# A decoder trunk on one core: the first up pair of the MLP in the wide form

## Chip, cores and metric

One core of a Trainium2 chip runs the whole program. The metric is device time in microseconds (us). The kernel before took 1468.94 us (median of 3 runs, 1468.91 to 1469.76).

## What is computed

Two decoder layers on 512 tokens of width 1024, all in 32-bit floats, and a last RMSNorm. In each layer an attention branch and a retention branch are merged, and an MLP follows. The change is in the MLP:

```python
def hybrid_layer(x, g_mix, w_in, sinks, w_a, w_b, w_out, g_mlp, w_up, w_down):
    ...
    x = x + mixed @ w_out
    h2 = rmsnorm(x, g_mlp)
    x = x + jnp.square(jax.nn.relu(h2 @ w_up)) @ w_down     # w_up: 1024 x 4096
    return x
```

## The kernel before

Activations lie with features on the partitions and the 512 tokens along the free dimension. The 32-bit product is made of three matmuls on split numbers: each operand is `hi` (a rounded copy, made by ScalarE) plus `lo` (the rest, made by VectorE), and hi·hi, hi·lo and lo·hi are summed in PSUM (`products`, L332 to L334).

**Weights.** They come in units of 128x1024 from one long list. `unit()` hands over the next one and has the two behind it split already: SyncE loads `raw` (L196, or L219 for the parked pairs), ScalarE makes `hi` (L286), VectorE makes `lo` (L287). `raw`, `hi` and `lo` have three buffers each. So a `hi` can only be made when TensorE has read the `hi` that held its buffer, and a `raw` can only be loaded when the `lo` of the unit before it in that buffer has been made.

**The up product.** The 32 chunks of 128 columns of w_up go so: four in one `group` (four PSUM banks, full width), then fourteen pairs of chunks. A pair computes a 2x2 block product with seven block products in place of eight (a Strassen form): blocks are 512 features by 256 tokens. It takes four units, and holds three PSUM banks named b, a and e, in this order: a from an input block; b starts as a copy of a; e from a sum of blocks ("form"); b and a each go on accumulating; b and e each once more; b a last time, for which its readers must be done. Each of these seven products is called a multiply below: four pieces of 128 rows.

There are two forms of the pair. `narrow_pair` writes 256 columns per matmul, three matmuls per piece (12 per multiply). `wide_pair` puts the moving hi and lo side by side as 512 columns: one matmul of 512 columns with the weights' hi (L1356 before the change) and one of 256 with their lo (L1357), so 8 matmuls per multiply. It leaves two halves in PSUM that must be added: copies of e and b are 512 wide (`eu`, L1386, and `bu`, L1390, ScalarE), the copy of a into b too (L1383), and `join` and `join_copied` add the halves on VectorE (L1362 and L1363, L1367 to L1369). Then VectorE applies relu and the RMS factor to all 512 tokens of both chunks (L1409), ScalarE squares (L1429), and the result is split (L339, L340).

`pair` picks the form by the chunk number c = 8q + 2i with `wide(c)`. Before, `FIRST_WIDE` is 6: the first pair of a layer (c = 4) is narrow and the other thirteen are wide. The first wide pair on the second PSUM pool (c = 8) starts with one matmul more (L1381), which writes the whole bank b once. The four chunks of the group are still in PSUM when the first pair begins: they need the RMS factor `rstd` (L464 to L472), which is only ready then. Their evacuation (L1333, L1334, then the split L339 and L340) is handed to the first pair, whose steps issue it between its own (`late`).

**Order.** A scheduler of the build orders the instructions of each engine; on the chip each engine takes them in that order. The pairs of one layer and the down products between them (`two_chunks`, which use the squared results) are interleaved by it.

Of the kernel before, what the change touches and what calls it, by code (L numbers as in the profile page):

```python
# [14 lines left out]
ALU = mybir.AluOpType  # L15
# [3 lines left out]
P = 128  # L19
# [29 lines left out]
DEEP = 3  # L49
DELAY = 2  # L50
ASIDE = 48
FIRST_WIDE, LAST_WIDE = 6, 32
BETWEEN = (0, 2, 4, 5)
PARKED = (("w_b", 0), ("w_b", 2), ("w_out", 6), ("w_up", 4), ("w_up", 6))
H = T // 2
# [37 lines left out]
def wide(chunk):  # L93

    return FIRST_WIDE <= chunk < LAST_WIDE
# [32 lines left out]
def decoder(ctx, tc, xT, x_first, w_in, w_a, w_b, w_out, w_up, w_down, tables, decay, band, triangles, g_last, out):  # L128
    nc = tc.nc
# [13 lines left out]
    def temp(name="t"):  # L143
        return tmp.tile([P, T], F32, tag="t", name=name)

    def big(name, dtype=F32):
        return tmp.tile([P, 2, T], dtype, tag="big", name=name, bufs=7)

    def bank(pool, name):
        return pool.tile([P, T], F32, tag=pool.name, name=name)  # L150
# [141 lines left out]
    def unit(name, layer):  # L292
        i = state["next"]
        assert order[i][:2] == (layer, name), (order[i], layer, name)
        state["next"] += 1
        split_until(i + 3)
        return parts.pop(i)
# [28 lines left out]
    def products(ps, pairs, start, stop, resume=False):  # L326


        n = len(pairs)
        for i, ((ah, al), (bh, bl)) in enumerate(pairs):  # L330
            more = {"skip_group_check": True} if resume else {}
            nc.tensor.matmul(ps, ah, bh, start=start and i == 0, stop=False, **more)  # L332
            nc.tensor.matmul(ps, ah, bl, start=False, stop=False, **more)  # L333
            nc.tensor.matmul(ps, al, bh, start=False, stop=stop and i == n - 1, **more)  # L334

    def split(hi, lo, src, scale=None):

        if scale is None:
            nc.scalar.activation(hi, src, AF.Copy)  # L339
            nc.vector.tensor_tensor(lo, src, f32(hi), ALU.subtract)  # L340
        else:
            nc.scalar.activation(hi, src, AF.Copy, scale=scale)  # L342
            nc.vector.scalar_tensor_tensor(lo, src, scale, f32(hi), ALU.mult, ALU.subtract)
# [58 lines left out]
    def all_of(steps):  # L402
        for step in steps:
            step()
# [198 lines left out]
    def layer_body(layer):  # L603
        g_mix, g_mlp = 2 * layer, 2 * layer + 1
        rms_mix, rms_mlp = Rms(g_mix, True), Rms(g_mlp, False)
# [4 lines left out]
        def forms_home():  # L610

            t = slots.four()
            form = t[0].rearrange("p a (b t) -> p (a b) t", t=H).rearrange("p (j k s) t -> p j k s t", k=2, s=2)
            return t, form
# [27 lines left out]
        def form_of(by_form):  # L642
            return lambda j: [by_form[2 * (j // 2) + k // 2][:, j % 2, k % 2, :, :] for k in range(4)]

        def block(half, tokens):
            at = slice(tokens * H, tokens * H + H)
            return [x_homes[k // 2][0][:, k % 2 :: 2, at] for k in range(4 * half, 4 * half + 4)]
# [3 lines left out]
        def narrow_pair(pool, step, form, block, put):  # L651
            def multiply(ps, weights, left, moving, start=True):
                hi, lo = weights
                cols = [slice((0 if left else 4 * P) + k * P, (0 if left else 4 * P) + (k + 1) * P) for k in range(4)]
                pairs = [((hi[:, c], lo[:, c]), m if isinstance(m, tuple) else (m[:, 0, :], m[:, 1, :])) for c, m in zip(cols, moving)]
                products(ps, pairs, start, True, not start)

            b, a, e = (bank(pool, "mm")[:, :H] for _ in range(3))
            eu, z = temp("eu"), big("z")
            part = unit("pair", layer)  # L660
            multiply(a, part, True, block(0, 0))
            ins = nc.scalar.activation(b, a, AF.Copy).ins
            step(ins)
            multiply(e, part, False, form(0))
            ins = nc.scalar.activation(eu[:, :H], e, AF.Copy).ins
            step(ins)
            part = unit("pair", layer)
            multiply(b, part, True, form(1), False)
            ins = nc.scalar.activation(eu[:, H:], b, AF.Copy).ins
            step(ins)  # L670
            multiply(a, part, False, block(1, 0), False)
            step(put(0, FIRST, a, z).ins)
            part = unit("pair", layer)
            multiply(b, part, True, form(2), False)
            ins = nc.vector.tensor_tensor(z[:, 1, SECOND], b, eu[:, :H], ALU.add).ins
            step(ins)
            multiply(e, part, False, block(1, 1), False)
            ins = nc.vector.tensor_tensor(z[:, 0, SECOND], e, eu[:, H:], ALU.add).ins
            step(ins)
            part = unit("pair", layer)  # L680
            multiply(b, part, True, form(3), False)
            put(slice(0, 2), SECOND, z[:, :, SECOND], z)
            put(1, FIRST, b, z)
            return z
# [474 lines left out]
        for u in range(4):  # L1159
            hi, lo = unit("w_a", layer)  # L1160
            for j in range(2):
                c = 2 * u + j
# [144 lines left out]
        for c in range(2, KD, 2):  # L1307
            pool = ps_mm if c == 4 else ps_aux
# [6 lines left out]
            slots.give(*t[1])  # L1315


        def positive(i, at, src, z):
            factor = rms_mlp.value[:, at]
            if not isinstance(i, int):  # L1320
                factor = factor.unsqueeze(1).broadcast_to([P, 2, H])
            return nc.vector.scalar_tensor_tensor(z[:, i, at], src, 0.0, factor, ALU.max, ALU.mult)

        homes_x = [forms_home() for _ in range(4)]
        by_form = [h[1] for h in homes_x]
        form = form_of(by_form)
# [13 lines left out]
        def up_home():  # L1340

            if any(len(f) == 4 for f in slots.free):
                t, own = slots.four()
                return t[:, 0:2, :], t[:, 2:4, :], own
            return big("uhi", F32R), big("ulo", F32R), []
# [66 lines left out]
        def pair(q, i, late):  # L1412

            c = 8 * q + 2 * i
            pool = ps_aux if i % 2 == 0 else ps_mm
            turn = iter(range(7))

            def step(ins):
                now = next(turn)
                while late and now == BETWEEN[4 - len(late)]:  # L1420
                    with tc.issue_after(ins), tc.issue_after(last_low[0]):
                        late.pop(0)()

            z = wide_pair(c == FIRST_WIDE + 2, i == 0 and q > 1, pool, step) if wide(c) else narrow_pair(pool, step, form, block, positive)
            all_of(late)
            late.clear()
            hi, lo, own = up_home()
            for i in range(2):
                nc.scalar.activation(z[:, i, :], z[:, i, :], AF.Square)  # L1429
                split(hi[:, i, :], lo[:, i, :], z[:, i, :])  # L1430
                up[q].append((hi[:, i, :], lo[:, i, :]))
            up_slots[q].extend(own)
# [52 lines left out]
    for layer in range(DEPTH):  # L1485
        layer_body(layer)
# [181 lines left out]
```

## Time and profile before

| | |
|---|---|
| median of 3 runs | 1468.94 us (1468.91 to 1469.76) |
| span of the profiled execution | 1467.5 us |
| TensorE busy (matmuls) | 1461.0 us, 100% |
| VectorE busy | 1161.6 us, 79% |
| ScalarE busy | 814.6 us, 56% |
| DMA, mean | 135 GB/s |

The profiled execution's own time is its span; the runs' median lies 1.4 us above it, for what lies around the program. How to read the rows: PE is TensorE, PEld its weight loads, DVE is VectorE, ACT is ScalarE, SPq is the queue of SyncE that issues the DMAs. A row of the timeline has the start in us, the length in us, engine, line, operation, output<-input, shape, and xN where N like instructions were merged. L12 is line 12 of the kernel. Lengths overlap: the next instruction of an engine starts before the last one's length is over, so what an instruction costs in a full queue is the distance from one start to the next. A matmul's end is modelled. In what follows that distance is called its step.

The two layers run the same program, so places come in twos. The first pair of the first layer lies at 423.6 to 436.4 us, that of the second 727.9 us later.

### The profile page before, as it was taken

Reading aid. Unit: us, or ns where it says so; the run is one execution under the profiler, and the core shown is the slowest. Engines: PE = TensorE matmul, PEld = TensorE weight load, DVE = VectorE, ACT = ScalarE, POOL = GpSimd, SP = SyncE. Lnnn points to the kernel's source line nnn. Section 1 sums busy time; section 2 is a strip of 40 time slices with the busy share of each in tenths; the row PEclk is TensorE's granted clock in tenths of the full one; section 3 lists DMA queues with packets and bytes.
Section 4 is the critical chain, followed back from the end, with each engine's and each line's share of the span. In section 5 each row is a group of like instructions: output and inputs, shape, how many; then the busy total and the mean of one; then the engine's idle time right before and its main releaser. Section 6 shows DMA issues by size and latency. Waiting matters only on the chain.

```text
span 1467.5 us, 20166 instructions
## 1 busy us (share of the span) xinstructions
PE 1461.0 (100%) x7434; PEld 1246.4 (85%) x7434; DVE 1161.6 (79%) x1912; ACT 814.6 (56%) x1306; POOL 3.7 (0%) x14
## 2 busy tenths in 40 slices
PE   9999999999999999999999999999999999999998
PEld 7888888888988888888888888888989888888887
DVE  7998778678988787776678977786899877877774
ACT  7657356654684445444456653666547754455544
POOL 0000000000000000000000000000000000000000
PEclk9999999999999999999999999999999999999999
DMA  6423843356443332333543258323654432333373
GB/s 227 134 87 101 280 166 98 104 171 210 130 120 125 101 115 88 107 108 115 165 121 102 86 168 285 107 95 107 191 197 123 144 101 87 125 105 101 108 200 108
DMA packets 73346, 198.65 MB, mean 135 GB/s; under 512 B 8712, under 2 KB 8864, under 8 KB 73248
## 3 DMA queue, kind: packets, MB, share of 16 engines
q1 hardware_dynamic: 72960, 196.84, 42.5%
q8 instruction: 58, 0.95, 0.3%
q10 hardware_dynamic: 288, 0.52, 0.1%
q14 instruction: 40, 0.33, 0.1%
HBM read 173.73 MB, written 20.98 MB: 133 GB/s over the span
## 4 chain that ended last, share of the span: by engine, by line
PE 99%; DVE 0%; issue 0%; POOLq 0%; ACT 0%; DVEq 0%; ACTq 0%
PE mm L334 24%; PE mm L332 23%; PE mm L333 23%; PE mm L1356 11%; PE mm L1357 6%; PE rv L332 2%; PE rv L334 2%; PE rv L333 2%; PE score L864 1%; PE r L332 1%; PE r L334 1%; PE r L333 1%; PE pT L819 0%; PE pv L846 0%; PE pv L845 0%; PE warm L311 0%
## 5 line engine op out<-in xcount | busy, mean ns | idle before, releaser
L333 PE MATMUL mm<-r,hi 128*128 128x512 f32 (+1 forms) x1568 | 572.5, 367 | 0.0
L332 PE MATMUL mm<-r,hi 128*128 128x512 f32 (+1 forms) x1568 | 569.9, 367 | 0.0
L334 PE MATMUL mm<-r,lo 128*128 128x512 f32 (+1 forms) x1568 | 563.9, 367 | 0.2
L286 ACT ACTIVATE hi<-raw 128x1024 fp32r<-128x1024 f32 (+1 forms) x334 | 333.9, 1002 | 377.8 <-PE mm L333 206.9
L287 DVE TENSOR_TENSOR lo<-raw,hi 128x512 fp32r<-128x512 f32 (+1 forms) x335 | 384.3, 1150 | 110.8 <-ACT hi L286 109.4
L334 PEld LDWEIGHTS mm<-r,lo 128*128 128x128 f32 x1568 | 293.6, 188 | 48.8 <-DVE lo L287 1.4
L332 PEld LDWEIGHTS mm<-r,hi 128*128 128x128 f32 x1568 | 294.1, 188 | 46.5 <-ACT r L342 0.2
L333 PEld LDWEIGHTS mm<-r,hi 128*128 128x128 f32 x1568 | 294.3, 188 | 46.0
L1356 PE MATMUL mm<-r,hi 128*128 128x512 f32 x728 | 252.0, 391 | 0.0
L1357 PE MATMUL mm<-r,lo 128*128 128x256 f32 x728 | 200.3, 277 | 0.0
L1356 PEld LDWEIGHTS mm<-r,hi 128*128 128x128 f32 x728 | 136.5, 188 | 28.7 <-ACT mm L1383 0.2
L1357 PEld LDWEIGHTS mm<-r,lo 128*128 128x128 f32 x728 | 136.7, 188 | 3.2 <-DVE lo L287 0.6
L1429 ACT ACTIVATE z<-z 128x512 f32<-128x512 f32 x56 | 32.5, 624 | 51.8 <-DVE z L1409 51.8
L1436 DVE TENSOR_TENSOR x<-x,mm 128x512 f32<-128x512 f32 x56 | 37.7, 686 | 28.1 <-PE mm L334 28.1
L334 PE MATMUL rv<-hi,r 128*128 128x512 f32 x128 | 49.8, 389 | 0.0
L333 PE MATMUL rv<-lo,r 128*128 128x512 f32 x128 | 49.8, 389 | 0.0
L332 PE MATMUL rv<-hi,r 128*128 128x512 f32 x128 | 49.8, 390 | 0.0
L339 ACT ACTIVATE r<-z 128x512 fp32r<-128x512 f32 x64 | 38.5, 619 | 16.3 <-DVE z L1090 16.1
L340 DVE TENSOR_TENSOR r<-z,r 128x512 fp32r<-128x512 f32 x64 | 42.9, 685 | 4.7 <-ACT r L339 4.3
L891 ACT ACTIVATE sm<-sm,st 128x256 f32<-128x256 f32 (+1 forms) x64 | 30.1, 472 | 19.0 <-DVE st L879 18.8
L1409 DVE SCALAR_TENSOR_TENSOR z<-z,rstd 128x512 f32<-128x512 f32 x52 | 35.6, 685 | 0.6
L340 DVE TENSOR_TENSOR r<-sums,r 128x1024 fp32r<-128x1024 f32 x24 | 28.9, 1216 | 0.0
(270 smaller groups left out, 1679.2 us busy)
## 6 DMA issues: line engine op xcount, KB each, us to landing
raw<-w_in_in SPq DMA_DIRECT2D x89, 512.0 KB, 3.6
raw<-w_down_in SPq DMA_DIRECT2D x64, 512.0 KB, 3.6
raw<-w_up_in SPq DMA_DIRECT2D x32, 512.0 KB, 3.9
raw<-w_up_in SPq DMA_DIRECT2D x60, 256.0 KB, 2.9
raw<-w_a_in SPq DMA_DIRECT2D x8, 512.0 KB, 6.5
ahead<-w_b_in SPq DMA_DIRECT2D x8, 512.0 KB, 5.4
park_w_b<-ahead SPq DMA_DIRECT2D x16, 256.0 KB, 5.9
ahead<-w_up_in SPq DMA_DIRECT2D x8, 512.0 KB, 5.7
```

Source lines behind the costliest of these rows:

```text
L286: nc.scalar.activation(hi[:, at], raw[:, at], AF.Copy)
L287: last_low[:] = [nc.vector.tensor_tensor(lo[:, at], raw[:, at], f32(hi[:, at]), ALU.subtract).ins]
L332: nc.tensor.matmul(ps, ah, bh, start=start and i == 0, stop=False, **more)
L333: nc.tensor.matmul(ps, ah, bl, start=False, stop=False, **more)
L334: nc.tensor.matmul(ps, al, bh, start=False, stop=stop and i == n - 1, **more)
L339: nc.scalar.activation(hi, src, AF.Copy)
L340: nc.vector.tensor_tensor(lo, src, f32(hi), ALU.subtract)
L1356: nc.tensor.matmul(both, hi[:, c], m, start=start and k == 0, stop=False, **more)
L1357: nc.tensor.matmul(ps[:, :H], lo[:, c], m[:, 0, :], start=False, stop=k == 3 and start, **more)
L1409: nc.vector.scalar_tensor_tensor(z[:, :, at], z[:, :, at], 0.0, factor, ALU.max, ALU.mult)
L1429: nc.scalar.activation(z[:, i, :], z[:, i, :], AF.Square)
L1436: nc.vector.tensor_tensor(x[:, c, :], x[:, c, :], ps, ALU.add)
```

## The change

The first pair (c = 4) takes the wide form. Its starting matmul that writes the bank b, which stood in the pair with c = 8, now stands in the pair with c = 4 (c == FIRST_WIDE). The helper `positive`, which only the narrow up pair used, goes. The split units of that pair are laid out as those of the other wide pairs (`first = (ASIDE, 0)`).

```diff
-FIRST_WIDE, LAST_WIDE = 6, 32
+FIRST_WIDE, LAST_WIDE = 4, 32
...
-        def positive(i, at, src, z):
-            factor = rms_mlp.value[:, at]
-            if not isinstance(i, int):
-                factor = factor.unsqueeze(1).broadcast_to([P, 2, H])
-            return nc.vector.scalar_tensor_tensor(z[:, i, at], src, 0.0, factor, ALU.max, ALU.mult)
-
...
-            z = wide_pair(c == FIRST_WIDE + 2, i == 0 and q > 1, pool, step) if wide(c) else narrow_pair(pool, step, form, block, positive)
+            z = wide_pair(c == FIRST_WIDE, i == 0 and q > 1, pool, step)
```

Six lines are gone, so what was L1333 is L1327 in the changed kernel, and so on. The scheduler orders the instructions anew. Outside of the stretch from the first pair of each layer to the third, the order is as before. Three places in that stretch follow; numbers behind names tell buffers apart.

**VectorE, second half of the first pair.** `up` are the group's chunks, `lo_4059` and `lo_4101` are the first and second unit of the pair behind (the second pair). Before:

```order
L287 TENSOR_TENSOR lo_4059<-raw_3979,hi_4058 128x1024 [waits DMAHW1_49,DMAHW2_49,DVE_49,Activation_49]
L340 TENSOR_TENSOR r7_83<-up_4037,r7_83 128x512 [waits Activation_49]
L675 TENSOR_TENSOR z_3978<-mm_3974,eu_3977 128x256 [waits PE_49]
L1333 SCALAR_TENSOR_TENSOR up_4075<-mm_3801,rstd_3885 128x512
L1333 SCALAR_TENSOR_TENSOR up_4093<-mm_3802,rstd_3885 128x512
L287 TENSOR_TENSOR lo_4101<-raw_4017,hi_4100 128x1024 [waits DMAHW3_49,DMAHW4_49,DVE_49,Activation_49]
```

The same place now; `lo_4047` and `lo_4085` are the first and second unit of the second pair, mm_3974, mm_3975 and mm_3976 are b, a and e of the first:

```order
L287 TENSOR_TENSOR lo_4047<-raw_3980,hi_4046 128x1024 [waits DMAHW1_49,DVE_49,DMAHW2_49,PE_49,Activation_49]
L1327 SCALAR_TENSOR_TENSOR up_4061<-mm_3801,rstd_3885 128x512 [waits DVE_49]
L1362 TENSOR_TENSOR bu_3978<-bu_3978,mm_3976 128x256 [waits DVE_49,PE_49]
L1357 TENSOR_TENSOR z_3979<-mm_3975,side_4040 128x256 [waits Activation_49]
L340 TENSOR_TENSOR r7_83<-up_3997,r7_83 128x512 [waits Activation_49]
L1362 TENSOR_TENSOR eu_3977<-eu_3977,mm_3974 128x256 [waits PE_49]
L340 TENSOR_TENSOR r7_83<-up_4027,r7_83 128x512 [waits Activation_49]
L1363 TENSOR_TENSOR z_3979<-mm_3976,bu_3978 128x256 [waits DVE_49]
L1327 SCALAR_TENSOR_TENSOR up_4077<-mm_3802,rstd_3885 128x512 [waits DVE_49]
L287 TENSOR_TENSOR lo_4085<-raw_4011,hi_4084 128x1024 [waits DMAHW4_49,DMAHW3_49,Activation_49]
L1363 TENSOR_TENSOR z_3979<-mm_3974,eu_3977 128x256 [waits DVE_49]
```

Between the two units stood four instructions, now eight.

**TensorE, the end of the first pair's last multiply.** Before, it stood after one multiply of the second pair. Now it stands after four, and its end is followed at once by the first down product (mm_4218, mm_4219), whose weights are `hi_4167`:

```order
L1351 MATMUL mm_3974<-r3_79,lo_4015 128x256
L1350 MATMUL mm_3974<-r3_79,hi_4014 128x512
L1351 MATMUL mm_3974<-r3_79,lo_4015 128x256
L332 MATMUL mm_4218<-r7_83,hi_4167 128x512 [waits Activation_49]
L333 MATMUL mm_4218<-r7_83,hi_4167 128x512
L332 MATMUL mm_4219<-r7_83,hi_4167 128x512
L333 MATMUL mm_4219<-r7_83,hi_4167 128x512
L1350 MATMUL mm_4109<-r5_81,hi_4115 128x512 [waits Activation_49]
```

Before, the second pair's remaining multiplies stood ahead of the first down product, here mm_4235 with `hi_4184`:

```order
L1357 MATMUL mm_4124<-r3_79,lo_4133 128x256
L1356 MATMUL mm_4124<-r3_79,hi_4132 128x512
L1357 MATMUL mm_4124<-r3_79,lo_4133 128x256
L332 MATMUL mm_4235<-r7_83,hi_4184 128x512 [waits Activation_49]
L333 MATMUL mm_4235<-r7_83,hi_4184 128x512
```

Four matmuls of the down product are now in front of the second pair's fifth multiply.

**ScalarE, the units for these.** `hi_4115` and `hi_4139` are the third and fourth unit of the second pair. `hi_4167` takes the buffer of `hi_4014`, the unit of that last multiply, so the TensorE wait in its row is for the end of it:

```order
L286 ACTIVATE hi_4115<-raw_4043 128x1024 [waits DMAHW6_49,DMAHW5_49,PE_49]
L1328 ACTIVATE up_4077<-up_4077 128x512 [waits DVE_49]
L339 ACTIVATE r4_80<-up_4077 128x512 [waits Activation_49]
L286 ACTIVATE hi_4139<-raw_4082 128x512 [waits DMAHW7_49,DVE_49,PE_49]
L286 ACTIVATE hi_4167<-raw_4113 128x1024 [waits DMAHW0_49,PE_49]
L1356 ACTIVATE side_4097<-mm_3974 128x256 [waits PE_49]
```

Before, the unit that followed into the buffer of the first pair's last one was the second pair's third, which TensorE asked for four multiplies later; now it is the next that TensorE asks for.

## Prediction

> **What bounds the kernel now.** The page first: its span, its first section and the chain that ended last (shares of the span).
>
> ```profile
> span 1467.5 us, 20166 instructions
> PE 1461.0 (100%) x7434; PEld 1246.4 (85%) x7434; DVE 1161.6 (79%) x1912; ACT 814.6 (56%) x1306; POOL 3.7 (0%) x14
> PE 99%; DVE 0%; issue 0%; POOLq 0%; ACT 0%; DVEq 0%; ACTq 0%
> ```
>
> TensorE is the bound from end to end, so a change gains what it takes from TensorE's queue, and loses whatever makes that queue wait. Whether it can wait is read where the change is, not from averages. Two windows hold the first pair (first row) and most of the second (PE, PEld, DVE, ACT and POOL busy, then granted clock, DMA share, GB/s):
>
> ```profile
> 424.00:436.00 12.00, 12.00 (x96) 11.44 (x96) 10.88 (x15) 10.85 (x21) 0.00 (x0) 1.00 0.37 110
> 436.00:448.00 12.00, 12.00 (x63) 10.05 (x62) 11.10 (x20) 7.72 (x14) 0.00 (x0) 1.00 0.67 207
> ```
>
> Against 79% over the span VectorE is at 10.88 and 11.10 of 12 us here, ScalarE at 10.85 of 12 in the first. The reason is the place: the group's four chunks can only be evacuated once the RMS factor is there, in the midst of this pair. The wide form adds work on just these two engines.
>
> **What it takes from TensorE.** The timeline of TensorE: first and last matmul of the narrow pair's first six multiplies, one multiply of the second pair, the narrow pair's seventh, and the second pair again.
>
> ```profile
> 423.60 0.28 PE L332 MATMUL mm<-r,hi 128*128 128x256 f32 x1
> ...
> 431.97 0.28 PE L334 MATMUL mm<-r,lo 128*128 128x256 f32 x1
> 432.08 0.40 PE L1356 MATMUL mm<-r,hi 128*128 128x512 f32 x1
> 432.48 0.39 PE L1357 MATMUL mm<-r,lo 128*128 128x256 f32 x1
> ...
> 436.10 0.39 PE L1356 MATMUL mm<-r,hi 128*128 128x512 f32 x1
> 436.33 0.28 PE L1357 MATMUL mm<-r,lo 128*128 128x256 f32 x1
> 436.44 0.62 PE L1356 MATMUL mm<-r,hi 128*128 128x512 f32 x2
> ...
> 439.19 0.43 PE L1356 MATMUL mm<-r,hi 128*128 128x512 f32 x1
> ```
>
> 72 narrow matmuls take 432.08 − 423.60 = 8.48 us, 0.118 each, 0.354 for the three of a piece. A wide piece goes from 436.10 to 436.44: 0.23 for the 512 columns, 0.11 for the 256, 0.34 in all. The pair has 28 pieces: 28 x 0.014 = 0.4 us less per layer. That is small because both forms stream 768 columns per piece.
>
> The Trainium skill ("TensorE: Matmul & The Clock Gate", section "Back-to-back issue gap") gives N/2.4 + 2.5 ns for a warm matmul of N columns. By it a narrow piece would take 327.5 ns and a wide one 325, so the saving would be 0.07 us per pair. The rows above disagree in the spacing (118 ns where the page has 109), and I go by them; either way it is below what decides here.
>
> The starting matmul of bank b (one of 512 columns, a step of 0.23) is moved from the third pair to the first, and costs nothing in sum. One wait of before goes too: 432.08 to 432.48 is 0.40 where the step is 0.23, so 0.17 us was lost there, for `lo_4059`.
>
> **What it adds to VectorE and ScalarE.** Rows of VectorE from `rstd` on, before the change:
>
> ```profile
> 427.85 0.69 DVE L1333 SCALAR_TENSOR_TENSOR up<-mm,rstd 128x512 f32<-128x512 f32 x1 [0.69 <-ACT rstd L472]
> 428.51 0.69 DVE L287 TENSOR_TENSOR lo<-raw,hi 128x512 fp32r<-128x512 f32 x1
> 429.12 0.68 DVE L1333 SCALAR_TENSOR_TENSOR up<-mm,rstd 128x512 f32<-128x512 f32 x1
> 429.72 0.41 DVE L1322 SCALAR_TENSOR_TENSOR z<-mm,rstd 128x256 f32<-128x256 f32 x1
> ...
> 431.21 1.22 DVE L287 TENSOR_TENSOR lo<-raw,hi 128x1024 fp32r<-128x1024 f32 x1
> ...
> 434.51 1.22 DVE L287 TENSOR_TENSOR lo<-raw,hi 128x1024 fp32r<-128x1024 f32 x1
> ...
> 442.72 0.42 DVE L1369 TENSOR_TENSOR z<-mm,bu 128x256 f32<-128x256 f32 x1
> 443.06 0.41 DVE L1363 TENSOR_TENSOR z<-mm,side 128x256 f32<-128x256 f32 x1
> 443.39 0.41 DVE L1368 TENSOR_TENSOR eu<-eu,mm 128x256 f32<-128x256 f32 x1
> 443.71 0.68 DVE L340 TENSOR_TENSOR r<-z,r 128x512 fp32r<-128x512 f32 x1
> 444.32 1.22 DVE L287 TENSOR_TENSOR lo<-raw,hi 128x1024 fp32r<-128x1024 f32 x1
> 445.45 0.42 DVE L1369 TENSOR_TENSOR z<-mm,eu 128x256 f32<-128x256 f32 x1
> ```
>
> The two middle rows are the second pair's units: `lo_4059` is done at 431.21 + 1.22 = 432.43, TensorE goes on at 432.48 (0.05 for the wait's release); `lo_4101` is done at 435.73, and TensorE asks for it only behind the two matmuls that start at 436.44, at 436.9. The last six rows lie back to back and give the steps: 0.33 for a 256-wide add, 0.61 for 512, 1.13 for a unit. The narrow pair has two adds and two factors of 256 and one factor of 512 (4 x 0.33 + 0.61 = 1.93), the wide one eight adds and two factors of 512 (8 x 0.33 + 2 x 0.61 = 3.86): 1.9 us more on an engine with 1.1 us free in the window.
>
> Now I lay the changed order on these steps, from where it first differs. ScalarE's rows:
>
> ```profile
> 426.12 1.70 ACT L472 ACTIVATE rstd<-own 64x256 f32<-64x256 f32 x4 [0.34 <-DVE own L469]
> 427.85 0.63 ACT L286 ACTIVATE hi<-raw 128x512 fp32r<-128x512 f32 x1
> ...
> 437.97 0.62 ACT L1429 ACTIVATE z<-z 128x512 f32<-128x512 f32 x1
> 438.49 0.58 ACT L1386 ACTIVATE eu<-mm 128x512 f32<-128x512 f32 x1
> 438.97 0.62 ACT L1429 ACTIVATE z<-z 128x512 f32<-128x512 f32 x1
> ...
> 440.49 1.06 ACT L286 ACTIVATE hi<-raw 128x1024 fp32r<-128x1024 f32 x1
> 441.44 0.38 ACT L1362 ACTIVATE side<-mm 128x256 f32<-128x256 f32 x1
> ```
>
> Steps: 0.52 for 512, 0.48 from PSUM, 0.95 (1.06 to its end) for a unit. `rstd` and the 512 behind it stand as before; then `eu` from 428.38, `bu` 428.86, a square 429.34, and `hi_4046` 429.86 to 430.92. VectorE: two group chunks and a half unit as before until 429.72, two adds of 256, then `lo_4047` from 430.95 to 432.17. TensorE's six multiplies with the starting matmul end at 423.60 + 24 x 0.34 + 0.23 = 431.99, so it needs `lo_4047` at 432.22: just met, and the 0.17 goes.
>
> *Wait A.* Behind `lo_4047` VectorE has eight instructions, four of 256 and four of 512: 4 x 0.33 + 4 x 0.61 = 3.76. So `lo_4085` starts at 430.95 + 1.13 + 3.76 = 435.84 and is done at 437.06. TensorE does two multiplies of the second pair (8 pieces, 8 x 0.34 = 2.72, to 434.71) and two matmuls of 512 columns, to 435.16, and waits for it until 437.11: 1.95 us. Queued behind are the rest of two multiplies (2.72 − 0.45 = 2.27) and the first pair's last one (1.36): TensorE is through at 440.74. Before, the same work, the first pair and four multiplies of the second, was through at 439.19. Net 1.55 us, the 0.4 and the 0.17 included, since TensorE now goes by VectorE's time.
>
> *Wait B.* The next row is the down product with `hi_4167`, whose buffer is that of the unit just being read. The last read of that hi starts at 440.74 − 0.34 = 440.40 and takes 0.39; ScalarE, idle by then, begins at 440.82 and ends at 441.88; TensorE starts at 441.93: 1.19 us. Before, two multiplies stood there (439.19 + 2.72). The second pair's fifth multiply could run, but stands behind it in the queue. It needs `eu` of the second pair, two instructions behind `hi_4167` (0.95 + 0.38 + 0.58, to 442.7 at most), and the four down matmuls cover that until 441.93 + 0.91 = 442.84. From there TensorE has two multiplies and most of the down unit without a wait that these rows show. What VectorE has left over behind may cost 0 to 0.5 us more per layer; I take 0.
>
> Sum per layer: 1.55 + 1.19 − 0.23 (the starting matmul, which the third pair no longer has) = 2.5 us. The second layer stands alike: its unit that answers to 434.51 is this one, 727.89 us later.
>
> ```profile
> 1162.40 1.22 DVE L287 TENSOR_TENSOR lo<-raw,hi 128x1024 fp32r<-128x1024 f32 x1
> ```
>
> Two layers: 5.0 us on the span of 1467.5, and 1468.94 + 5.0 = **1474.0 us** against the median, which lies 1.4 above the span for work that doesn't change.
>
> **Transfers.** The raw of `hi_4167` may be loaded when `lo_4085` is done, at 437.1. Such loads land after
>
> ```profile
> raw<-w_down_in SPq DMA_DIRECT2D x64, 512.0 KB, 3.6
> raw<-w_a_in SPq DMA_DIRECT2D x8, 512.0 KB, 6.5
> ```
>
> 3.6 us in the median: 440.7, with 0.1 us of cover against 440.82. Before, it could start when `lo_4101` was done, at 435.73, and the unit was split at 440.49. The slowest weight row of that size, 6.5, would land at 443.6 and lengthen B by 2.8 us per layer. I take the first, of the very tensor; the second is the end of the range.
>
> **Rivals.**
> 1. *Not slower: both waits hidden.* VectorE's adds would have to make `lo_4085` ready by 435.16, 1.9 us earlier, half of the 3.76 between the units. Then the gain alone is left: 2 x (0.4 + 0.17), about 1467.8. For it speaks only that a scheduler chose this order; against it that 0.33 and 0.61 are steps of the same instructions in the same trace. It decides from a step of half the size. Chance 0.08.
> 2. *Only A.* If ScalarE could split `hi_4167` early, 2 x (1.55 − 0.23): 1471.6. Against it: three buffers, and the read of `hi_4014` ends with the multiply. Chance 0.10.
> 3. *Late transfers.* B grows by up to 2.8: between 1475 and 1479.6. For it: the cover is 0.1 us. Chance 0.20.
> 4. *The clock.* If the granted clock fell in the waits, matmuls would run at half speed for a while, as they do at the start, where the ten matmuls of 512 columns below are 0.46 us apart against 0.23:
>
> ```profile
> 1.04 4.63 PE warm L311 x10
> ```
>
> That many behind each wait would add 2.3 us per drop, 1478.6 for one per layer. Both windows above show 1.00, with no wait of this length in them. The Trainium skill (the same page, "Part 1: The HAM clock gate") has the clock fall after an idle window of about 3.4 us. Waits of 1.95 and 1.19 us are shorter, so by that rule it stays; no run here shows it yet. Chance 0.05.
> 5. *The change does not do what it says.* Then nothing moves, 1468.9. Against it: the changed order has the 512-wide matmuls in this pair. Chance 0.01.
>
> **How the numbers follow.** Forecast 0.56, rivals as above. A measurement of this kernel tells 0.2% (2.9 us) from no change, so same is 1466.0 to 1471.9. Most of rival 1 falls there (0.06), half of 2 (0.05), rival 5 and a little of the forecast (0.02): same 0.13. No row gives 2.9 us back, so only 0.02 of rival 1 is faster. The rest is slower, 0.85. The range goes from A alone (1471.4) to late transfers with part of the rest (1478.0).
>
> **What would show it.** TensorE's timeline would have a gap of about 1.9 us near 435.2 released by VectorE's `lo` (L287), and one of 1.2 near 440.8 by ScalarE's `hi` (L286), again 728 to 731 us later; VectorE full from 430.9 to 441. The 28 pieces at 0.34 would show the gain. Wrong would be the forecast if the second unit's `lo` ended before 435.2, if the gap at `hi` is released by the DMA, or if the loss stood elsewhere.

## The result, and the profile after

The changed kernel took **1475.09 us** (median of 4 runs, 1474.41 to 1475.34) beside 1469.20 for the kernel before (median of 4 runs, 1468.91 to 1469.76): a ratio of 1.0040, 95% interval 1.0028 to 1.0051. So it is slower, by 5.9 us; its profiled execution has a span of 1473.1 us against 1467.5, 5.6 more. The forecast was 1474.0. Page of the changed kernel: span, busy time, shares of the chain that ended last.

```profile
span 1473.1 us, 20064 instructions
PE 1461.1 (99%) x7378; PEld 1243.3 (84%) x7378; DVE 1165.8 (79%) x1922; ACT 817.6 (56%) x1310; POOL 3.7 (0%) x14
PE 97%; DVE 1%; ACT 1%; issue 1%; POOLq 0%; DVEq 0%; ACTq 0%
```

VectorE and ScalarE have 4 and 3 us more work in 1473, which by itself says little. What tells is that they now appear on the chain, with 1% each. The table of TensorE's waits names who was waited for (total, times, longest; left out is the row of the program's start, the only one that the kernel before has):

```profile
PE mm L1351 <- DVE lo L287: 3.2, 2, 1.6
PE mm L332 <- ACT hi L286: 2.1, 2, 1.0
```

Two waits, each twice, once per layer. TensorE's timeline of the changed kernel, from the first pair's first matmul, shows where:

```profile
423.42 0.40 PE L1350 MATMUL mm<-r,hi 128*128 128x512 f32 x1
...
434.64 0.65 PE L1350 MATMUL mm<-r,hi 128*128 128x512 f32 x2
436.90 0.38 PE L1351 MATMUL mm<-r,lo 128*128 128x256 f32 x1 [1.61 <-DVE lo L287]
437.12 0.40 PE L1350 MATMUL mm<-r,hi 128*128 128x512 f32 x1
...
440.34 0.39 PE L1350 MATMUL mm<-r,hi 128*128 128x512 f32 x1
440.56 0.28 PE L1351 MATMUL mm<-r,lo 128*128 128x256 f32 x1
441.87 0.50 PE L332 MATMUL mm<-r,hi 128*128 128x512 f32 x1 [1.03 <-ACT hi L286]
442.21 0.40 PE L333 MATMUL mm<-r,hi 128*128 128x512 f32 x1
...
465.15 0.40 PE L334 MATMUL mm<-r,lo 128*128 128x512 f32 x1
465.64 0.51 PE L332 MATMUL mm<-r,hi 128*128 128x512 f32 x1
465.98 0.39 PE L333 MATMUL mm<-r,hi 128*128 128x512 f32 x1
```

The bracket counts idle time from a matmul's modelled end. What a wait costs is the distance of starts less the usual step. *Wait A*: the second of the two merged matmuls starts at 434.90 (434.64 + 0.65 − 0.39), the next at 436.90: 2.00 less 0.23 is 1.77 us; so TensorE asked at 435.13. *Wait B*: 441.87 − 440.56 − 0.11 = 1.20. A third, *wait C*: 465.64 − 465.15 − 0.23 = 0.26. The matmul behind a wait also has a longer step by 0.11 (436.90 to 437.12 is 0.22 in place of 0.11; 441.87 to 442.21 and 465.64 to 465.98 are 0.34 in place of 0.23).

VectorE of the changed kernel, the second pair's first unit (`lo_4047`), the first and the last of the eight instructions behind it, and the second unit (`lo_4085`):

```profile
430.76 1.22 DVE L287 TENSOR_TENSOR lo<-raw,hi 128x1024 fp32r<-128x1024 f32 x1 [0.48 <-ACT hi L286]
431.91 0.68 DVE L1327 SCALAR_TENSOR_TENSOR up<-mm,rstd 128x512 f32<-128x512 f32 x1
...
435.04 0.68 DVE L1327 SCALAR_TENSOR_TENSOR up<-mm,rstd 128x512 f32<-128x512 f32 x1
435.63 1.21 DVE L287 TENSOR_TENSOR lo<-raw,hi 128x1024 fp32r<-128x1024 f32 x1
```

The second unit ends at 436.84, TensorE goes on at 436.90. ScalarE of the changed kernel, the units for B and C, each with the idle time ahead of it and the TensorE matmul that released it:

```profile
440.76 1.06 ACT L286 ACTIVATE hi<-raw 128x1024 fp32r<-128x1024 f32 x1 [0.73 <-PE mm L1350]
...
464.52 2.01 ACT L286 ACTIVATE hi<-raw 128x1024 fp32r<-128x1024 f32 x2 [3.23 <-PE mm L1350]
```

In both ScalarE stood idle until TensorE had read the buffer, and the copy then took 1.06 (at C it is the first of the two merged rows). At B TensorE waited for all of it; at C it had other matmuls to do meanwhile and waited for the last 0.26. And the two windows, to compare with those of before:

```profile
424.00:436.00 12.00, 11.29 (x65) 9.52 (x63) 10.68 (x17) 11.76 (x22) 0.00 (x0) 1.00 0.38 110
436.00:448.00 12.00, 10.07 (x53) 8.47 (x54) 10.05 (x18) 7.32 (x13) 0.00 (x0) 1.00 0.56 175
```

TensorE, 12.00 in both before, misses 0.7 and 1.9 us. The granted clock stays at 1.00.

The loss lies in this stretch. From the first pair's start to one and the same matmul behind the third pair, in the kernel before (its start is 423.60):

```profile
474.40 0.39 PE L334 MATMUL mm<-r,lo 128*128 128x512 f32 x1
```

and in the changed one:

```profile
477.12 0.39 PE L334 MATMUL mm<-r,lo 128*128 128x512 f32 x1
```

50.80 against 53.70: 2.90 us for the first layer. Two times 2.9 is 5.8; the changed kernel's profiled execution came to the pair 0.18 us earlier, where the order of the instructions is still the same, and that leaves the 5.6 of the spans.

### The profile page after: what moved, and what is told of

Its sections match the earlier page's. It is cut to its first block, busy times and chain, and to the rows that moved or that the text cites. A ratio compares the mean times of both kernels' runs of the same rounds, so it can differ in the third digit from the quotient of the medians.

```text
span 1473.1 us, 20064 instructions
## 1 busy us (share of the span) xinstructions
PE 1461.1 (99%) x7378; PEld 1243.3 (84%) x7378; DVE 1165.8 (79%) x1922; ACT 817.6 (56%) x1310; POOL 3.7 (0%) x14
## 4 chain that ended last, share of the span: by engine, by line
PE 97%; DVE 1%; ACT 1%; issue 1%; POOLq 0%; DVEq 0%; ACTq 0%
PE mm L332 23%; PE mm L334 23%; PE mm L333 23%; PE mm L1350 11%; PE mm L1351 6%; PE rv L332 2%; PE rv L334 2%; PE rv L333 2%; PE score L864 1%; PE r L332 1%; PE r L334 1%; PE r L333 1%; PE pT L819 0%; ACT hi L286 0%; PE pv L845 0%
## 5 line engine op out<-in xcount | busy, mean ns | idle before, releaser
L333 PE MATMUL mm<-r,hi 128*128 128x512 f32 (+1 forms) x1512 | 556.8, 370 | 0.0
L332 PE MATMUL mm<-r,hi 128*128 128x512 f32 (+1 forms) x1512 | 554.0, 371 | 2.2 <-ACT hi L286 2.1
L334 PE MATMUL mm<-r,lo 128*128 128x512 f32 (+1 forms) x1512 | 548.2, 370 | 0.2
L332 PEld LDWEIGHTS mm<-r,hi 128*128 128x128 f32 x1512 | 283.8, 188 | 50.0 <-ACT hi L286 3.7
L333 PEld LDWEIGHTS mm<-r,hi 128*128 128x128 f32 x1512 | 283.9, 188 | 45.6
L1350 PE MATMUL mm<-r,hi 128*128 128x512 f32 x784 | 271.1, 390 | 0.0
L1351 PE MATMUL mm<-r,lo 128*128 128x256 f32 x784 | 216.1, 277 | 3.2 <-DVE lo L287 3.2
L1350 PEld LDWEIGHTS mm<-r,hi 128*128 128x128 f32 x784 | 147.0, 188 | 30.9 <-ACT mm L1377 0.2
```

Source lines behind the costliest of these rows:

```text
L1350: nc.tensor.matmul(both, hi[:, c], m, start=start and k == 0, stop=False, **more)
L1351: nc.tensor.matmul(ps[:, :H], lo[:, c], m[:, 0, :], start=False, stop=k == 3 and start, **more)
```

## Experiments

The theory: A is VectorE's queue between the two units, B is the `hi` buffer that is read until the moment its successor is needed, and nothing else is behind the loss. The main rivals: the amount of VectorE's work in this stretch, whatever its order; TensorE's own order; late transfers; something of the whole program. Spans are of one profiled execution each, beside 1467.5 for before and 1473.1 for the changed kernel; ratios are of medians against the kernel before, with their 95% interval. The time of a run lies 1.7 to 2.2 us above the span of the same run, so times are compared with times and spans with spans. Kernels built on the one before have its line numbers.

**One layer alone (`one_layer`).** The kernel before, with the wide pair in layer 0 only.

```diff
-if paired and order[i][4] == "w_up" and wide(order[i][2]):
+if paired and order[i][4] == "w_up" and (wide(order[i][2]) or (order[i][0] == 0 and order[i][2] == 4)):
...
-z = wide_pair(c == FIRST_WIDE + 2, i == 0 and q > 1, pool, step) if wide(c) else narrow_pair(...)
+z = wide_pair(c == (FIRST_WIDE - 2 if layer == 0 else FIRST_WIDE + 2), ...) if wide(c) or (layer == 0 and c == 4) else narrow_pair(...)
```

> The kernel before, with the first pair in the wide form in the first layer alone (the starting matmul too). If the loss is made at this pair's place and nowhere else, half of it is left: a span of 1470.3 (1467.5 and 5.6 halved), with the waits of 1.77 and 1.19 us at 435 and 441 us and none 731 us later. If something of the whole program is to blame (the layout of the units, code that differs, the clock), the span would lie away from the middle, at 1467.5 or 1473.

Measured: 1469.9, ratio 1.0019 (1.0009 to 1.0028). TensorE's waits of this kernel:

```profile
PE mm L1357 <- DVE lo L287: 1.6, 1, 1.6
...
PE mm L332 <- ACT hi L286: 1.0, 1, 1.0
```

Each wait comes once, of the same length. So the loss is made at this pair, by layer.

**VectorE's order.** In `own_steps` a step of the first pair hands on the pair's own add, so that the group's late evacuations stand behind it:

```diff
-                nc.vector.tensor_tensor(dest, ps[:, :H], side, ALU.add)
+                return nc.vector.tensor_tensor(dest, ps[:, :H], side, ALU.add).ins
...
-            join(z[:, 0, :H], a)
-            step(ins)
+            own = join(z[:, 0, :H], a)
+            step(own if first else ins)
```

(the same at the next two joins). In `own_2345` the evacuations also begin a step later:

```diff
-BETWEEN = (0, 2, 4, 5)
+BETWEEN = (2, 3, 4, 5)
```

> The changed kernel, where three steps of the first pair hand on the pair's own add in place of the copy ahead of it, so that the group's late evacuations stand behind these adds. VectorE's work is the same to the instruction; only their order differs, and two instructions fewer stand between the second pair's first and second unit. If wait A is the queue between the two units, it falls from 1.77 us to about 0.6, B stays at 1.2 and the third wait stays at 0.3: span 1470.7. If it is the amount of VectorE's work in this stretch, whatever its order, nothing changes: 1473.1.

> The kernel of own_steps, and the group's late evacuations begin one step later (BETWEEN 2, 3, 4, 5 in place of 0, 2, 4, 5). VectorE's work is again the same; its queue between the second pair's first and second unit gets shorter by one 512-wide instruction. By the queue between the units A falls to 0.2 us, B stays at 1.2, the third at 0.3: span 1469.8. If what own_steps gained came from something else than this queue, the span stays at own_steps' 1470.8 (its 1471.7 less 0.9 us of a late transfer in its first layer alone), or goes up.

Measured: `own_steps` 1471.7, ratio 1.0030 (1.0017 to 1.0042), 1.0 us above what was expected; `own_2345` 1469.5, ratio 1.0017 (1.0008 to 1.0026). A is 0.59 us in the first and 0.23 in the second, in both layers; B stays at 1.20 in both. TensorE's instructions stand in the same order as in the changed kernel, in `own_steps` all of them, in `own_2345` as far as the first down product's second unit. The two units on VectorE in `own_steps`:

```profile
430.87 1.23 DVE L287 TENSOR_TENSOR lo<-raw,hi 128x1024 fp32r<-128x1024 f32 x1 [0.48 <-ACT hi L286]
...
434.54 1.22 DVE L287 TENSOR_TENSOR lo<-raw,hi 128x1024 fp32r<-128x1024 f32 x1
```

They start 3.67 us apart, against 4.87 in the changed kernel: 1.20 less, and A fell by 1.18. VectorE's instructions are the same in kind and number. That decides for the queue and against the amount of work, with TensorE's order held. The 1.0 us that `own_steps` has too much lies elsewhere: in its first layer a load of w_up landed late, in the second it didn't (VectorE, first instruction on that load in each layer):

```profile
447.24 0.69 DVE L252 TENSOR_TENSOR raw<-raw 128x512 f32<-128x512 f32 x1 [1.72 <-DMA raw<-w_up_in]
...
1176.59 0.69 DVE L252 TENSOR_TENSOR raw<-raw 128x512 f32<-128x512 f32 x1 [0.57 <-DMA raw<-w_up_in]
```

The first is 1.15 us longer, and TensorE lost 0.86 between 450 and 454 us that it didn't lose in the second layer. The six runs of this kernel have spans from 1470.4 to 1473.0 us, so the load may be late in some of them and not in others; why, is open.

**The amount of VectorE's work (`narrow_more`).** The kernel before, with six adds of 256 columns more in the first pair (here the first of them; their result is not used):

```diff
+            def extra(*srcs):
+                for src in srcs if more else ():
+                    nc.vector.tensor_tensor(junk[:, :H], eu[:, :H], src, ALU.add)
```

> The kernel before, narrow pair, with six more adds of 256 columns on VectorE in the first pair, whose result is thrown away: the amount of VectorE work of the wide form (1.9 us more per layer), while TensorE's work and its order and the split units' early places stay. If the amount of VectorE's work in this stretch is the cause of A, the loss is like A's: 1.5 us per layer, a span of 1470.5. If it is what stands between the two units, it is 0.5 per layer at most: 1468.5.

Measured: 1468.6, ratio 1.0008 (0.9999 to 1.0018). There is no wait at the second unit. In the first layer TensorE loses 0.40 at a down unit's `hi` and 0.23 at a `lo`, in the second 0.43 at a `lo`. So with this work the span is 1.1 us longer, half a microsecond per layer. But this run doesn't tell VectorE's order from TensorE's: with the narrow pair, TensorE does the pair's last multiply ahead of the second unit, and asks for that unit at 437.23; VectorE has it ready at 436.36 (435.14 + 1.22):

```profile
436.76 0.62 PE L1367 MATMUL mm<-r,hi 128*128 128x512 f32 x2
437.23 0.28 PE L1368 MATMUL mm<-r,lo 128*128 128x256 f32 x1
```

In the changed kernel it asks at 435.13, 2.1 us earlier, mostly because that multiply (1.36) was put behind. A is thus made on two sides: a `lo` that comes 1.1 us later than before (436.84 against 435.73) and a request that comes 1.8 us earlier (435.13 against 436.9), where before left 1.2 us of room. A kernel with only the multiply moved back was not tried; the next run comes near it.

**Less work in the wide form (`wide_less`).** The changed kernel, in which the first pair leaves out two of the three adds of each copied join. (The half of two products that stands in the upper columns is left out.)

```diff
-                nc.vector.tensor_tensor(u[:, :H], u[:, :H], u[:, H:], ALU.add)
-                nc.vector.tensor_tensor(u[:, :H], u[:, :H], ps[:, H:], ALU.add)
+                if not first:
+                    nc.vector.tensor_tensor(u[:, :H], u[:, :H], u[:, H:], ALU.add)
+                    nc.vector.tensor_tensor(u[:, :H], u[:, :H], ps[:, H:], ALU.add)
```

> The changed kernel, where the first pair leaves out two of VectorE's three adds in each join of a copied half (the half of two products that comes from the weights' hi and the activations' lo is left out): four adds of 256 columns fewer per layer, 1.3 us of VectorE in the stretch. By the queue between the units A falls by the part of it that stands there, to 0.7 us, or below if the first unit comes earlier too; B falls to 0.7 since ScalarE's order around it is another; span 1468.7. If A doesn't come from VectorE's instructions there, the span stays near 1473.

Measured: 1468.2, ratio 1.0008 (0.9999 to 1.0017). A is gone (0.1 us), which is less than was expected, and for another reason. TensorE's last matmuls ahead of the second unit's `lo`, and the two units on VectorE:

```profile
435.86 0.62 PE L1350 MATMUL mm<-r,hi 128*128 128x512 f32 x2
```

```profile
430.60 1.22 DVE L287 TENSOR_TENSOR lo<-raw,hi 128x1024 fp32r<-128x1024 f32 x1 [1.14 <-ACT hi L286]
...
435.14 1.22 DVE L287 TENSOR_TENSOR lo<-raw,hi 128x1024 fp32r<-128x1024 f32 x1
```

The units start 4.54 us apart, only 0.33 less than in the changed kernel, and the second ends at 436.36. But the scheduler ordered this kernel anew, and the first pair's last multiply stands ahead of the second unit again: TensorE asks at 435.86 + 0.62 − 0.39 + 0.23 = 436.32. Counted from the pair's first matmul (423.25 here), the unit comes 0.31 us earlier than in the changed kernel and the request 1.36 later, which is one multiply. B is gone too, because the new order puts the down product behind six multiplies of the second pair again, in place of four; what comes in its place is 0.5 us at a `lo` of the down unit. So this run doesn't weigh VectorE's work by itself. It shows the other side of A: with that multiply back in its place the wait goes, though VectorE's queue is nearly as long. And it says of B only that the place of the down product decides it.

**TensorE's order at B (`down_later`).** The changed kernel with the first down product held back until the second pair's next-to-last multiply.

```diff
-                two_chunks("w_down", layer, up[q], [put_down(2 * i), put_down(2 * i + 1)], turning)
+                with tc.issue_after(last_of_pair[0]) if (q, i) == (0, 0) else nullcontext():
+                    two_chunks("w_down", layer, up[q], [put_down(2 * i), put_down(2 * i + 1)], turning)
```

> The changed kernel with the first down product's matmuls held back until the second pair's next-to-last multiply. If wait B is only TensorE's own order (the fifth multiply of the second pair could run, but stands behind the down product), B goes and the span falls to 1470.7. If the ScalarE queue behind the unit's hi (the second pair's copy eu stands behind it) holds the fifth multiply too, TensorE waits there in place of it, for 2.0 us against 1.2: span about 1474.6.

Measured: 1478.9, ratio 1.0071 (1.0056 to 1.0086). TensorE's waits of this kernel:

```profile
PE mm L1350 <- ACT eu L1381: 3.6, 2, 1.8
PE mm L1351 <- DVE lo L287: 3.2, 2, 1.6
```

The fifth multiply now waits 1.95 us for `eu`, which stands on ScalarE behind the down unit's `hi`. So B is not TensorE's order alone: ScalarE's queue holds up the next best work as well. But the kernel is 4.3 us above what was expected by that, and the granted clock shows why (busy times as above, then the clock; why the windows have these borders is said at the next run):

```profile
436.60:440.01 3.41, 2.58 (x15) 2.33 (x16) 3.41 (x6) 1.17 (x3) 0.00 (x0) 1.00 0.46 133
440.01:443.43 3.42, 1.63 (x9) 1.20 (x9) 2.33 (x4) 2.69 (x5) 0.00 (x0) 1.00 0.70 206
443.43:446.84 3.41, 3.41 (x11) 2.84 (x11) 2.94 (x8) 1.70 (x5) 0.00 (x0) 0.50 0.73 232
```

Behind the second wait the clock was granted at half for 3.41 us: 1.7 us of clock lost. It is so in the second layer too. With the 0.75 by which the new wait is longer than B that is 2 x 2.45 = 4.9 of the 5.8 us above the changed kernel; a wait of 0.53 at 1401 us is most of the rest.

The same kernel doesn't always lose this. Three of its four runs have spans of 1478.0 to 1478.9 us and a mean granted clock of 0.997 or 0.998. The fourth has 1475.4 and 0.999, the clock of kernels in which it never fell: 3.5 us less than the profiled one, about twice 1.7.

**Is one such wait enough for the clock (`own_down_later`)?** Both edits together, so that A is short and the wait for `eu` stays.

> The two edits of own_steps and down_later together. In down_later TensorE waited 1.77 us (A), worked for 3.9 us, waited 1.95 us for the copy eu, and then the granted clock was 0.50 for some 3.5 us, which cost about 1.7 us more per layer. Here A is 0.6 and the wait for eu stays at 1.95. If that one wait is enough to make the clock fall, it falls again: own_steps without its late transfer, 1470.8, and 2 x (0.75 + 1.7): 1475.7. If it takes both waits, the clock stays at 1.00: 1472.3.

Measured: 1472.3, ratio 1.0039 (1.0026 to 1.0053). The wait for `eu` is 1.96 us in both layers, A is 0.60 and 0.53, and the clock stays at 1.00:

```profile
437.38:440.80 3.42, 2.02 (x12) 1.51 (x11) 3.42 (x6) 3.29 (x7) 0.00 (x0) 1.00 0.69 252
440.80:444.21 3.41, 3.02 (x16) 2.59 (x17) 3.38 (x8) 1.71 (x5) 0.00 (x0) 1.00 0.71 175
```

That is what was expected if it takes both waits, but it doesn't show it, because something else differs between the two kernels too. The traces hold the moments at which the clock changed. In `down_later` they lie 128, 1, 214, 1 and 87 times 3.413 us apart, and in the thirteen other traces the one stretch at full clock is 428 to 438 times as long, each time a whole number. So in these traces the clock changes only on a grid with steps of 3.41 us, which lies elsewhere in each execution. The windows of both kernels above are cut on it.

In `down_later` the whole wait for `eu` falls into one step, which is idle for 1.79 of its 3.41 us, in both layers, and the clock falls at its end. The step ahead of it is idle for 0.83 in the first layer and 0.09 in the second. In `own_down_later` a border of the grid cuts the same wait in two: the steps are idle for 1.40 and 0.39, in the second layer for 1.48 and 0.32. In all fourteen traces the most idle step between the first matmuls and the last behind which the clock stayed has 1.60 (`one_layer`, from 434.13). So the idle time of a single step tells every case apart, with the border between 1.60 and 1.79, and the fourth run of `down_later` fits it too, if its grid lay otherwise. Whether an earlier wait counts as well is not shown, and no run moves the grid against the waits. The other three runs of `own_down_later` have spans of 1473.1 to 1474.3 and a mean clock of 0.999; one fall of the clock in one of them can't be excluded.

**The buffer at B (`hi4_big6`, `hi4_big6_own`).** The changed kernel, and `own_steps`, with four `hi` buffers; the room is taken from a pool of temporary tiles and from the padding.

```diff
-        return tmp.tile([P, 2, T], dtype, tag="big", name=name, bufs=7)
+        return tmp.tile([P, 2, T], dtype, tag="big", name=name, bufs=6)
...
-wpool.tile([P, UNIT + P], F32R, tag=n, name=n)[:, a : a + UNIT]
+wpool.tile([P, UNIT + ASIDE], F32R, tag=n, name=n, bufs=4 if n == "hi" else 3)[:, a : a + UNIT]
```

> The changed kernel with four buffers for hi in place of three (the room is taken from a pool of temporary tiles, six in place of seven). Then the first down unit needs not wait for the read of the first pair's last unit. If wait B is the hi buffer, TensorE's wait released by the hi (L286) at 441 us goes to 0.2 us or less; wait A stays (the order differs a little, and a part of it may stand at the first unit). Laid on the steps the whole gives 2.5 us of waits per layer in place of 3.2: span about 1471.3. If B is not the buffer (ScalarE busy, or the transfer), the wait at L332 stays at 1.2 us.

> Both remedies together: four hi buffers, and the own adds first as in own_steps. If A is the VectorE queue between the units and B the hi buffer, and nothing else is behind the loss, nearly all of it goes: waits of 0.9 us per layer in all, a span of 1468.2, within 0.2 per cent of the kernel before. If a third cause of the size of A or B exists, the span stays above 1470.

Measured: 1499.5, ratio 1.0206 (1.0192 to 1.0220), and 1491.7, ratio 1.0178 (1.0164 to 1.0192). The spans are far above what was expected, but the place of B is there: the first down product stands right behind the first pair's last multiply, as in the changed kernel, with the same 89 matmuls of the two pairs ahead of it. In `hi4_big6`, the end of that multiply, the first down matmul, and the unit's `hi` on ScalarE:

```profile
446.88 0.28 PE L1351 MATMUL mm<-r,lo 128*128 128x256 f32 x1
447.00 0.40 PE L332 MATMUL mm<-r,hi 128*128 128x512 f32 x1
```

```profile
445.67 1.06 ACT L286 ACTIVATE hi<-raw 128x1024 fp32r<-128x1024 f32 x1 [1.32 <-PE mm L1350]
```

ScalarE makes the unit while the last multiply still runs, and TensorE goes on after 0.12 us, the usual step, in the second layer too; in `hi4_big6_own` 0.13 and 0.19 are left. So with a fourth buffer B is gone, as expected if it is the buffer. Wait A is not there to compare, because the scheduler's order is another; TensorE waits 0.42 for `eu` and 0.92 for the copy of a into b in its place (0.46 and 0.89 in the second layer). What the spans lose is elsewhere: the steps of TensorE's matmuls of 512 columns are longer all over the program. What made them longer was tried by itself (`pads`): the kernel before, the same instructions in the same order, with the padding alone changed.

```diff
-wpool.tile([P, UNIT + P], F32R, tag=n, name=n)[:, a : a + UNIT]
+wpool.tile([P, UNIT + ASIDE], F32R, tag=n, name=n)[:, a : a + UNIT]
```

> The kernel before, all instructions and their order the same; only the room of a split unit's buffer is 1072 columns in place of 1152, so that the buffers of hi and lo lie at other addresses. In hi4_big6, which had this too, the steps of TensorE's 512-wide matmuls went from 227 ns to 231 and above all over the program, and cost over 20 us. If that is the address, it is here too: a span of about 1490. If it came from the fourth buffer or the changed order, this run gives 1467.5.

Measured: 1488.9, ratio 1.0145 (1.0131 to 1.0159). 28 matmuls of 512 columns ahead of the first pair, first and last, in this kernel:

```profile
422.63 0.39 PE L333 MATMUL mm<-r,hi 128*128 128x512 f32 x1
...
428.90 0.40 PE L334 MATMUL mm<-r,lo 128*128 128x512 f32 x1
```

and the same 28 in the kernel before:

```profile
417.26 0.39 PE L333 MATMUL mm<-r,hi 128*128 128x512 f32 x1
...
423.38 0.39 PE L334 MATMUL mm<-r,lo 128*128 128x512 f32 x1
```

27 steps take 6.27 against 6.12 us: 232 ns each against 227, with no wait between. So the 21 us come from the narrower buffers, and with them most of what the fourth buffer seemed to cost. They move `hi` and `lo`, and also all temporary tiles, which are laid out behind them (6 buffers x 80 columns x 4 bytes = 1920 bytes lower); which of these addresses it is, and why, is open.

**The copy at B (`own_2345_halves2`).** With buffers and addresses left alone, `own_2345` with the split of two down units made in two halves:

```diff
-if i < 3 else (slice(0, UNIT),)
+if i < 3 or order[i][1:3] in (("w_down", 0), ("w_down", 2)) else (slice(0, UNIT),)
```

> The kernel of own_2345, and the hi and lo of two down units (the one behind wait B and the one behind the third wait) are made in two halves of 512 columns in place of one piece of 1024; buffers and transfers stay. If B is the copy that can begin only when its buffer is read, TensorE waits for the first half alone, and B falls from 1.2 us to about 0.8; the third wait, of 0.3, goes; 0.36 may come at the second pair's fifth multiply for the copies behind: 1.36 us per layer in place of 1.7, a span of 1468.8. If the transfer of the raw sets B, halves change nothing there: 1469.5 or above.

Measured: 1468.9, ratio 1.0011 (1.0002 to 1.0020). TensorE at B:

```profile
438.41 0.39 PE L1350 MATMUL mm<-r,hi 128*128 128x512 f32 x1
438.63 0.28 PE L1351 MATMUL mm<-r,lo 128*128 128x256 f32 x1
439.52 0.50 PE L332 MATMUL mm<-r,hi 128*128 128x512 f32 x1 [0.61 <-ACT hi L286]
```

and ScalarE, the two halves merged:

```profile
438.83 1.15 ACT L286 ACTIVATE hi<-raw 128x512 fp32r<-128x512 f32 x2 [0.17 <-PE mm L1350]
```

The buffer's last read ends at 438.41 + 0.39 = 438.80, the first half begins at 438.83, and TensorE goes on at 439.52: B is 0.77 in place of 1.20 in both layers, shorter by what half a copy is shorter. C is gone; 0.25 came at the fifth multiply. So B is the read of the buffer and then the copy, as the fourth buffer says too, and the transfer had no part in it.

**What the wide form gains where nothing waits (`calm_narrow`).** The kernel before, with chunks 22 and 23 narrow too.

```diff
-    return FIRST_WIDE <= chunk < LAST_WIDE
+    return FIRST_WIDE <= chunk < LAST_WIDE and chunk != 22
```

> The kernel before, with a later pair (chunks 22 and 23 of each layer) in the narrow form too. VectorE has room there. This shows the gain of the wide form by itself: 28 pieces of 0.014 us, 0.4 per layer, and a little more where the 512-wide adds are fewer: a span of 1468.3, 0.8 above before. If the wide form gains nothing on TensorE, 1467.5; if it gains by more than these steps say (a wait that the narrow form brings with it), above 1469.

Measured: 1467.8, ratio 1.0003 (0.9994 to 1.0012). A stretch round that pair, between the same two matmuls, in this kernel:

```profile
575.10 0.39 PE L332 MATMUL mm<-r,hi 128*128 128x512 f32 x1
...
673.05 0.39 PE L332 MATMUL mm<-r,hi 128*128 128x512 f32 x1
```

and in the kernel before:

```profile
575.12 0.39 PE L332 MATMUL mm<-r,hi 128*128 128x512 f32 x1
...
672.86 0.39 PE L332 MATMUL mm<-r,hi 128*128 128x512 f32 x1
```

97.95 against 97.74: the wide form gains 0.2 us in the first layer, half of what the steps give; with the narrow pair 0.2 us less was lost in that stretch to steps longer than the usual ones. The spans differ by 0.3, which leaves 0.1 for the second layer. The medians, 1469.69 and 1469.60, don't tell the two kernels apart. No version of the change was found that beats the kernel before, and with a gain of 0.1 to 0.4 per layer none could that this measurement would tell from no change.

## Why the prediction was right

The forecast's mechanism was what happened. Term by term, per layer:

- *The saving*, 28 x 0.014: the steps of the wide pieces are as predicted (0.34), so the term stands. In `calm_narrow`, at another pair, no more than 0.1 to 0.2 of it is left.
- *Wait A*, 1.95 predicted, 1.77 measured, released by VectorE's `lo` as said. Counted from the pair's first matmul, the unit ended when it should (13.42 us against 13.46): the eight steps of 0.33 and 0.61 were right. TensorE came to it 0.15 later (11.71 against 11.56), of which 0.09 lie at the first matmul that needs `lo_4047`: the unit was ready in time, but the step was 0.21 in place of 0.11. Net of the saving and the old wait: the first pair and four multiplies took 440.67 − 423.42 = 17.25, before 439.19 − 423.60 = 15.59, so 1.66 against 1.55. The difference is the 0.11 by which the matmul behind a wait steps longer. `own_steps` and `own_2345` show VectorE's side of the cause, `wide_less` TensorE's.
- *Wait B*, 1.19 predicted, 1.20 measured, and 0.11 behind it. `own_2345_halves2` and `hi4_big6` show the cause, and `down_later` that the fifth multiply was no way out, which the prediction had only read off the queue.
- *The starting matmul*, −0.23: moved, as said.
- *The rest*, "0 to 0.5", taken as 0: 2.90 − 1.66 − 1.31 + 0.23 = 0.16 were left over. This is the term that was mis-sized. It holds wait C (0.26 and 0.12 behind it, less small delays that went): beside the third pair a down unit's `hi` waits for its buffer just as at B. The prediction had looked for leftovers on VectorE, and this one stood on ScalarE.

Sum: 2.5 predicted, 2.9 measured. Of the 0.4 that are missing, 0.2 are the longer steps behind A and B, which no term held, and the other 0.2 are the rest. *Rival 1* (waits hidden) fell with the steps of VectorE. *Rival 2* (only A) fell with B. *Rival 3* (late transfers): ScalarE began the down unit at 440.76, when its buffer was read, so the load was there in time; one load of another unit came late in `own_steps`, in one layer. *Rival 4* (the clock) did not happen here; its price was put at 2.3 us per drop, and where it did happen it was 1.7. It was nearer than its chance of 0.05 says: in the profiled execution of `down_later` the second wait is 0.75 us longer, and the clock falls in both layers. The Trainium skill ("TensorE: Matmul & The Clock Gate", "Part 1: The HAM clock gate") lets the clock fall after an idle window of about 3.4 us. The changed kernel agrees with it: no step of the grid of 3.41 us is idle for more than 1.03, and the clock stays at 1.00. `down_later` does not, if the window has to be idle from end to end: 1.79 us of one step were enough. *Rival 5* falls with the 512-wide matmuls that the trace shows in the pair.

## What to carry to other kernels

Where one engine feeds the bound in order, count what stands between two of its deliveries, and when the bound asks for the second: A came from 1.1 us more on the one side and a request 1.8 us earlier on the other, and the same VectorE work in another order cost 0.23 in place of 1.77, with TensorE's order the same. A ring of buffers is as good as the order in which it is read: when a scheduler puts the reader of a buffer directly ahead of the user of its successor, the whole copy stands open on the bound (1.20 us; none with a fourth buffer, 0.77 when copied in halves). And a gain of 14 ns per piece is not worth moving work onto engines that are full at that place.

## What the runs showed of the hardware

- Where tiles lie sets TensorE's step for 512 columns: 227 ns with split buffers of 1152 columns, 232 with 1072 (the temporary tiles behind them moved too), 21 us over the program, with the same instructions in the same order. Which addresses do so, and why, is open.
- The granted clock changed only on a grid of 3.41 us, in fourteen traces. It fell to 0.50 for one step of the grid behind a step idle for 1.79 us (`down_later`, both layers), and stayed at 1.00 behind steps idle for 1.60 and less. One profiled execution of each kernel.
- The first matmul behind a wait has a step longer by 0.11 us, with 256 columns (0.22 in place of 0.11) and with 512 (0.34 in place of 0.23) alike.
